# Sums of weight blocks for a seven-product down projection: made by accumulating transfers in DRAM instead of by GpSimd in SBUF

## The chip, the core and the metric

One core of a Trainium2 chip runs the whole program. The metric is device time in microseconds. The kernel before takes 1990.42 us, the median of 3 runs (1988.92 to 1992.81). One more execution was taken with the profiler; all rows below are from that one.

Engines, as the profile names them: PE is the matrix engine (PEld its weight loads), DVE the vector engine, ACT the scalar engine, POOL is GpSimd, SP the engine that only issues transfers. SP, ACT and POOL each issue transfers on a queue of their own (q1, q10 and q0 in the profile), and all three queues are served by the same 16 DMA engines. Each engine works through its own instructions in order; an instruction that waits for a semaphore holds up all that stand behind it on that engine.

## What is computed

Two layers, each a token mixer and a gated channel MLP, on x of 512 tokens by 1024 channels, float32:

```python
for i in range(DEPTH):                       # DEPTH = 2
    mix = mixer_sublayer(x, w_in[i], ...)    # input projection, pooling mixer, SSD mixer, gates, w_out
    x = layer_norm(ALPHA * x + mix, ...)
    h = dwconv_centred(x @ w_up[i], ...)     # 1024 -> 2 * 2816
    gate, val = split(h)
    x = layer_norm(ALPHA * x + (gelu(gate) * val) @ w_down[i], ...)   # 2816 -> 1024
```

The change concerns the last product, (512 x 2816) @ (2816 x 1024), and only the way in which its weights are prepared.

## The kernel before

**Matmuls in three parts.** Every float32 operand of the big products is split into a rounded part h and a remainder l; `mm3` (L378 to L383) issues three matmuls, h·h, h·l, l·h. The split of a weight tile (`WeightStream._split`, L77 to L92) is an ACT cast (L90, `wh`) and a DVE subtraction (L91, `wl`) of 128 x 1024 values.

**The weight stream.** A plan lists raw loads of up to 1 MB (`wraw`, two buffers) and the order in which their pieces are split. SP issues the loads, `_split` cuts them two tiles ahead of PE, three `wh`/`wl` buffers hold them.

**The down projection with seven products.** `strassen_projection` (L604) multiplies 2 x 2 blocks of activations and weights with seven products instead of eight (Strassen's scheme in Winograd's form). The 2816 rows of `w_down` are 22 row blocks of 128; each of the 11 pairs has two row blocks and two halves of 512 columns, so four blocks b00, b01, b10, b11 per pair. Four products need sums of these blocks. Before the change `StrassenWeights` (L107) makes them on POOL when a pair's tile has been loaded: per pair three subtractions of 128 x 512 (L137, L138 in place in the loaded tile, L126 into the space of the old activations, `xths`/`xtls`), and later, for two pairs at once, one subtraction of 128 x 1024 (L154). The raw load of a pair has b00, b01 and b11 (768 KB); b10 comes later in three loads of up to 1 MB.

The stage has two parts: in the first, PE does four products for each of 11 pairs (24 matmuls a pair), while the other activation sums come back from DRAM (`asp`, `fetch` L618) and are cut again (`cut` L621, L624 and L625); in the second, the remaining three products.

**What sets the order of the work around the change.** PE's program order is the order of the source. The other engines' order is set by the framework's scheduler, which places an instruction where it takes the engine to be free and its inputs to be there; it may move one far ahead of the place where it was written. In the mixer, POOL makes the decay masks (`affine_select` of `m`, L994; `m` is loaded from DRAM on ACT's queue, L989), and per unit of four heads `xw` (L1051), `y` (L1057), state products `s` (L1076) and the sums into `y` (L1109). ACT exponentiates `m` (L1001) after the masks. PE's state product `stp` (L1068) reads `xw`, its `ydp` (L1019) reads `m`, its `yop` (L1095) reads `s`. In names like `m_0_775` the first number is the head, in `xw_0_826`, `y_0_829` and `s_0_2_921` the unit; the last one only numbers the buffer.

Of the kernel before, what the change touches and what calls it, by code (L numbers as in the profile page):

```python
# [9 lines left out]
F32 = mybir.dt.float32  # L10
# [3 lines left out]
ALU = mybir.AluOpType  # L14
# [3 lines left out]
P = 128  # L18
T = 512
D = 1024  # L20
KD = D // P
# [17 lines left out]
class WeightStream:  # L39
# [3 lines left out]
    def __init__(self, nc, tc, pool, plan, ahead, raw_bufs, bufs):  # L43
        self.nc, self.tc, self.pool = nc, tc, pool
        self.plan = plan
        self.subs = [(i, j) for i, r in enumerate(plan) for j in r["order"]]
        self.ahead = ahead
        self.raw_bufs, self.bufs = raw_bufs, bufs
        self.raw = {}
        self.done = {}  # L50
        self.next_raw = 0
        self.next_sub = 0
        self.pos = 0
        self.seq = []
        self.extra = {}
# [51 lines left out]
class StrassenWeights:  # L107
# [4 lines left out]
    def __init__(self, nc, tc, pairs):  # L112
        self.nc, self.tc, self.pairs = nc, tc, pairs
        self.t2 = {}
        self.raw0 = None

    def open(self, tiles):

        for t in tiles:
            for i in range(t.shape[1]):  # L120
                self.t2[len(self.t2)] = (t, i)
        self.make_t2(0, self.raw0)

    def make_t2(self, i, raw):
        t, j = self.t2[i]
        self.nc.gpsimd.tensor_tensor(  # L126
            t[:, j, :], raw[:, 1024:1536], raw[:, 512:1024], op=ALU.subtract
        )

    def direct(self, raw):  # L130

        return raw.rearrange("p (a b) -> p a b", a=2)[:, :, 0:512]

    def sums(self, i, raw):

        g = self.nc.gpsimd
        g.tensor_tensor(raw[:, 1536:2048], raw[:, 1024:1536], raw[:, 512:1024], op=ALU.subtract)  # L137
        g.tensor_tensor(raw[:, 512:1024], raw[:, 512:1024], raw[:, 0:512], op=ALU.subtract)  # L138
        if i:
            self.make_t2(i, raw)  # L140
        else:
            self.raw0 = raw
        return raw.rearrange("p (a b) -> p a b", a=2)[:, :, 512:1024]

    def two(self, q):
        t, j = self.t2[2 * q]
        return t[:, j : j + min(2, self.pairs - 2 * q), :]

    def lower(self, q, o, raw):

        t = self.two(q)
        n = t.shape[1]
        b = raw[:, o : o + n * 512].rearrange("p (a b) -> p a b", a=n)
        self.nc.gpsimd.tensor_tensor(t, b, t, op=ALU.subtract)  # L154
        return b

    def plan(self, w, first):

        raws, direct, sums = [], [], []
        for i in range(self.pairs):  # L160
            a, b = 2 * i * P, (2 * i + 1) * P
            raws.append({"srcs": [w[a : a + P, :].unsqueeze(1),
                                  w[b : b + P, 512:1024].unsqueeze(1)], "order": range(2)})
            direct.append((first + i, self.direct))
            sums.append((first + i, partial(self.sums, i)))
        seq = []
        for i in range(self.pairs - 2):
            seq += [direct[i], sums[i]]
        seq += direct[-2:] + sums[-2:]
        odd = w.rearrange("(k two p) c -> two p k c", two=2, p=P)[1, :, :, 0:512]  # L170
        lower, t2, t4 = [], [], []
        for i in range(0, self.pairs, 4):
            n = min(4, self.pairs - i)
            r = first + len(raws)
            raws.append({"srcs": [odd[:, i : i + n, :]], "order": range(n)})
            for k in range(0, n, 2):
                q = (i + k) // 2
                lower.append((r, partial(self.lower, q, k * 512)))
                t2.append((r if q else r - 1, lambda raw, q=q: self.two(q)))
                t4.append((r, lambda raw, q=q: self.two(q)))  # L180
        nq = len(t2)
        for q in range(nq - 2):
            seq += [t2[q], lower[q]]
        return raws, seq + t2[-2:] + lower[-2:] + t4
# [40 lines left out]
def weight_plan(l, w_in, pool_w, w_ssd_proj, w_out, w_up, w_down, down):  # L225
# [71 lines left out]
    r, s = down.plan(w_down[l], len(raws))  # L297
# [4 lines left out]
def tile_hybrid_pool_ssd_convffn_encoder(  # L302
# [60 lines left out]
    downs = [StrassenWeights(nc, tc, KF // 2) for _ in range(NL)]  # L363
# [134 lines left out]
    class Norm:  # L498
# [28 lines left out]
        def add(self, c, c0, ps, first=False, last=False):  # L527

            c1 = c0 + ps.shape[1]
            xs = self.xcs[c][:, c0:c1]  # L530
            if first:
                nc.vector.scalar_tensor_tensor(xs, xs, ALPHA, ps, op0=ALU.mult, op1=ALU.add)
            else:
                nc.vector.tensor_tensor(xs, xs, ps, op=ALU.add)
            if last:
                self.stats(c, c0, c1)
# [67 lines left out]
    def strassen_projection(l, name, sw, tags, pool, spill, norm):  # L604
# [13 lines left out]
        def fetch(i):  # L618
            nc.sync.dma_start(again[:, i % 2], spill[i])

        def cut(i):  # L621
            h = pool.tile([P, 4, 256], F32R, tag=f"ah{i}", name=f"{name}h{i}")
            lo = pool.tile([P, 4, 256], F32R, tag=f"al{i}", name=f"{name}l{i}")
            nc.scalar.copy(h[:, :3], again[:, i % 2])  # L624
            nc.vector.tensor_tensor(lo[:, :3], again[:, i % 2], h[:, :3], op=ALU.subtract)  # L625
            second[i] = (h, lo)
# [19 lines left out]
        for i in range(n - 2):  # L646
# [11 lines left out]
            fetch(i)  # L658
# [14 lines left out]
        for i in (n - 2, n - 1):  # L673
            both(yb, (tags[i], 1), s[i - n + 2], 0, False, i == n - 1)
            both(zb, (tags[i], 2), s[i - n + 2], 1, False, i == n - 1)
            fetch(i)
            cut(i - 1)
# [24 lines left out]
        with tc.high_priority():  # L702
            for cc in range(2):
                norm.add(cc, 512, xb[cc])
                norm.add(2 + cc, 512, xb[cc])
            if final:
                norm.add(3, 256, xb[1][:, 256:512])
# [60 lines left out]
    for l in range(NL):  # L768
# [483 lines left out]
        for g in range(4):  # L1252
# [88 lines left out]
        for j in range(KF):  # L1341
# [22 lines left out]
            nc.vector.tensor_tensor(q[:, 1], a21, r[:, 1], op=ALU.add)  # L1364
            nc.vector.tensor_tensor(q[:, 2], q[:, 0], a21, op=ALU.subtract)
            nc.vector.tensor_tensor(r[:, 2], q[:, 1], q[:, 0], op=ALU.subtract)
            nc.vector.tensor_tensor(q[:, 3], r[:, 0], r[:, 2], op=ALU.subtract)
# [57 lines left out]
```

## Time and profile before

| what | us |
|---|---|
| median of 3 runs | 1990.42 |
| profiled execution, its own time | 1992.83 |
| its span in the trace | 1991.0 |
| PE busy | 1931.9 (97%) |
| DVE busy | 1348.4 (68%) |
| ACT busy | 998.4 (50%) |
| POOL busy | 609.0 (31%) |

The span is one execution from its first to its last instruction; the stages follow each other in it: mixer of layer 0 to about 578 us, output projection and norm to about 636 us, up projection to 872 us, down projection to about 995 us, and the same again for layer 1, whose down projection runs from about 1868 us to the end. Idle time of an engine costs something only where the engine that sets the end waits for it.

### The profile page before, as it was taken

Reading aid. Unit: us, or ns where it says so; the run is one execution under the profiler, and the core shown is the slowest. Engines: PE = TensorE matmul, PEld = TensorE weight load, DVE = VectorE, ACT = ScalarE, POOL = GpSimd, SP = SyncE. Lnnn points to the kernel's source line nnn. Section 1 sums busy time; section 2 is a strip of 40 time slices with the busy share of each in tenths; the row PEclk is TensorE's granted clock in tenths of the full one; section 3 lists DMA queues with packets and bytes.
Section 4 is the critical chain, followed back from the end, with each engine's and each line's share of the span. In section 5 each row is a group of like instructions: output and inputs, shape, how many; then the busy total and the mean of one; then the engine's idle time right before and its main releaser. Section 6 shows DMA issues by size and latency. Waiting matters only on the chain.

```text
span 1991.0 us, 27368 instructions
## 1 busy us (share of the span) xinstructions
PE 1931.9 (97%) x10449; PEld 1616.0 (81%) x10449; DVE 1348.4 (68%) x1945; ACT 998.4 (50%) x1665; POOL 609.0 (31%) x578
## 2 busy tenths in 40 slices
PE   8999999999999999998999999999999999999997
PEld 7878798988888888876788878989888888888765
DVE  5668576775556656679985685667656566666898
ACT  4767666644333444444457776656443334444443
POOL 1244424241111111168303343242411111111773
PEclk9999999999999999999999999999999999999999
DMA  5444434233241334345225344343332414333541
GB/s 159 123 119 117 127 93 140 86 113 115 76 164 49 121 112 134 106 153 190 83 90 160 106 112 124 110 124 105 85 111 92 168 43 130 121 101 116 180 154 51
DMA packets 174691, 232.19 MB, mean 117 GB/s; under 512 B 7872, under 2 KB 128868, under 8 KB 174560
## 3 DMA queue, kind: packets, MB, share of 16 engines
q1 hardware_dynamic: 152144, 178.80, 28.3%
q10 hardware_dynamic: 17712, 34.08, 7.0%
q0 software_dynamic: 4704, 17.56, 2.5%
q8 instruction: 83, 1.36, 0.3%
q14 instruction: 48, 0.39, 0.1%
HBM read 217.31 MB, written 13.11 MB: 116 GB/s over the span
## 4 chain that ended last, share of the span: by engine, by line
PE 78%; DVE 6%; issue 6%; POOL 4%; DMA 3%; ACT 3%; SPq 0%; POOLq 0%; ACTq 0%; DVEq 0%
PE fg L382 7%; PE fg L381 7%; PE fg L383 7%; PE spp L381 3%; PE zp L381 3%; PE spp L382 3%; PE spp L383 3%; PE zp L382 3%; PE zp L383 3%; PE xp L381 3%; DVE wl L91 3%; PE xp L383 3%; PE xp L382 3%; PE stp L1068 2%; PE ydp L1019 2%
## 5 line engine op out<-in xcount | busy, mean ns | idle before, releaser
L91 DVE TENSOR_TENSOR wl<-wraw,wh 128x1024 fp32r<-128x1024 f32 (+1 forms) x330 | 454.1, 1377 | 251.6 <-ACT wh L90 250.0
L90 ACT CAST wh<-wraw 128x1024 fp32r<-128x1024 f32 (+1 forms) x330 | 341.2, 1035 | 503.6 <-PE fg L382 158.0
L383 PE MATMUL fg<-xthm,wl 128*128 128x512 f32 x640 | 249.0, 389 | 0.0
L381 PE MATMUL fg<-xthm,wh 128*128 128x512 f32 x640 | 249.0, 389 | 0.0
L382 PE MATMUL fg<-xtlm,wh 128*128 128x512 f32 x640 | 249.0, 389 | 0.0
L1001 ACT ACTIVATE m<-m,nac 128x128 f32<-128x128 f32 x512 | 159.6, 392 | 52.2 <-POOL m L994 51.7
L994 POOL TENSOR_SCALAR_AFFINE_SELECT m<-m 128x512 f32<-128x512 f32 x128 | 95.0, 765 | 183.5 <-DMA m<-acd 162.9
L381 PEld LDWEIGHTS fg<-xthm,wh 128*128 128x128 f32 x640 | 120.1, 188 | 25.0
L383 PEld LDWEIGHTS fg<-xthm,wl 128*128 128x128 f32 x640 | 120.1, 188 | 24.9
L382 PEld LDWEIGHTS fg<-xtlm,wh 128*128 128x128 f32 x640 | 120.1, 188 | 24.9
L1109 POOL TENSOR_TENSOR y<-y,yo 128x256 f32<-128x256 f32 x96 | 85.4, 898 | 101.6 <-DVE yo L1101 98.8
L381 PE MATMUL spp<-yth,wh 128*128 128x512 f32 x256 | 110.3, 431 | 0.5 <-ACT yth L1149 0.5
L382 PE MATMUL spp<-ytl,wh 128*128 128x512 f32 x256 | 101.2, 395 | 0.7 <-DVE ytl L1150 0.7
L383 PE MATMUL spp<-yth,wl 128*128 128x512 f32 x256 | 101.1, 395 | 0.0
L479 DVE SCALAR_TENSOR_TENSOR xc<-xp,pcwc,xc 128x510 f32<-128x510 f32 (+1 forms) x128 | 95.2, 745 | 7.2 <-ACT xc L473 5.7
L1002 DVE TENSOR_TENSOR m<-m 128x512 f32<-128x512 f32 x64 | 46.7, 730 | 64.8 <-ACT m L1001 55.5
L1051 POOL TENSOR_TENSOR xw<-xtok,wst 128x768 f32<-128x768 f32 x32 | 51.3, 1621 | 121.9 <-ACT xtok L943 99.0
L1363 POOL TENSOR_TENSOR r<-cvv,cg 128x512 f32<-128x512 f32 x22 | 28.4, 1292 | 175.1 <-issue 130.4
L381 PE MATMUL zp<-wh,xthf 128*128 128x256 f32 x256 | 77.6, 303 | 0.0
L1286 POOL TENSOR_TENSOR g<-g,acc 128x512 f32<-128x512 f32 x16 | 27.5, 1720 | 162.3 <-ACT g L1247 150.3
L381 PE MATMUL zp<-wh,xthi 128*128 128x256 f32 x256 | 77.1, 301 | 0.0
L382 PE MATMUL zp<-wl,xthf 128*128 128x256 f32 x256 | 73.0, 285 | 0.0
(403 smaller groups left out, 5214.0 us busy)
## 6 DMA issues: line engine op xcount, KB each, us to landing
wraw<-in_w_in_dram SPq DMA_DIRECT2D x56, 1024.0 KB, 5.5
wraw<-in_w_up_dram SPq DMA_DIRECT2D x44, 1024.0 KB, 5.2
m<-acd ACTq DMA_DIRECT2D x64, 512.0 KB, 4.9
wraw<-in_w_ssd_proj_dram SPq DMA_DIRECT2D x16, 1024.0 KB, 5.1
wraw<-in_w_down_dram SPq DMA_DIRECT2D x22, 512.0 KB, 3.6
asp<-r POOLq DMA_DIRECT2D x22, 384.0 KB, 2.9
xtls<-asp SPq DMA_DIRECT2D x22, 384.0 KB, 3.8
wraw<-in_w_in_dram SPq DMA_DIRECT2D x16, 512.0 KB, 5.3
```

The source lines that it names most:

```text
L90: self.nc.scalar.copy(hv, src)
L91: self.nc.vector.tensor_tensor(lv, src, hv, op=ALU.subtract)
L381: mm(lhsT=ah, rhs=bh, start=first, stop=False)
L382: mm(lhsT=ah, rhs=bl, start=False, stop=False)
L383: mm(lhsT=al, rhs=bh, start=False, stop=last)
L479: nc.vector.scalar_tensor_tensor(dst[:, o0:o1], ps[:, o0 + s : o1 + s], tap, dst[:, o0:o1], op0=ALU.mult, op1=ALU.add,)
L994: nc.gpsimd.affine_select(out=mv, in_=mv, pattern=[[0, NCH], [1 - 2 * d, P]], compare_op=ALU.is_ge, fill=NEG, base=0, channel_multiplier=2 ...
L1001: nc.scalar.activation(mc, mc, AF.Exp, bias=nac[:, c, col : col + 1])
L1002: nc.vector.tensor_tensor(m[:, 0], m[:, 0], m[:, 1], op=ALU.add)
L1019: nc.tensor.matmul(ps[q * 64 : (q + 1) * 64, c * 64 : (c + 1) * 64], lhsT=m[:, 0, t0 : t0 + 64], rhs=xtok[:, c, hh * 64 : (hh + 1) * 64], ...
L1051: nc.gpsimd.tensor_tensor(h4(xw[:, d]), h4(xtok[:, d : d + 3, :]), hb(wst, d, d + 3, d), op=ALU.mult)
L1109: nc.gpsimd.tensor_tensor(y[:, c, :], y[:, c, :], yo[:, d, :], op=ALU.add)
```

## The change

The sums of blocks are made before the stage needs them, in DRAM, by transfers that POOL issues and that add to what lies at their destination. `StrassenWeights.prepare(step)` is written in the mixer's loop over four groups: in step 0, four copies of all 11 blocks of a kind (b01, b01, b11, b10) to a DRAM tile `wsum`; in step 1, two accumulating transfers (b00 onto the first, b11 onto the second); in steps 2 and 3 one each, from one part of `wsum` onto another. Each transfer is 1408 rows of 2 KB, 2.88 MB; there are 8 per layer, 16 in all. The down projection then loads 1 MB per pair (b00, b11 and two sums), later one sum and b10 for two pairs at a time, and the last sum for four pairs. POOL does none of the sums any more. Since the transfers can only add, some sums have the other sign, and a few DVE instructions subtract where they added. The space of the old activations becomes two more raw buffers (`raw_at`) and five buffers for `asp` instead of two.

```diff
     def _load(self, i):
         r = self.plan[i]
-        raw = self.pool.tile([P, 2048], F32, tag="wraw", name=f"wraw{i}", bufs=self.raw_bufs)
+        if i in self.raw_at:
+            raw = self.raw_at[i]
+        else:
+            raw = self.pool.tile([P, 2048], F32, tag="wraw", name=f"wraw{i}",
+                                 bufs=self.raw_bufs)
...
-    def make_t2(self, i, raw):
...
-    def sums(self, i, raw):
...
-    def lower(self, q, o, raw):
...
+    def __init__(self, nc, w, pairs, sums):
+        self.nc, self.pairs, self.sums = nc, pairs, sums
+        self.blocks = w.rearrange("(k two p) (h c) -> two h p k c", two=2, h=2, p=P)
+
+    def _put(self, t, src, op=None):
+        dst = self.sums[:, :, t, :]
+        if op is None:
+            self.nc.gpsimd.dma_start(dst, src)
         else:
...
+            self.nc.gpsimd.dma_start(dst, src, accum_op=op)
+
+    def prepare(self, step):
+
+        b, t = self.blocks, self.sums
+        if step == 0:
+            for n, (i, j) in enumerate(((0, 1), (0, 1), (1, 1), (1, 0))):
+                self._put(n, b[i, j])
+        elif step == 1:
+            self._put(0, b[0, 0], ALU.add)
+            self._put(1, b[1, 1], ALU.add)
+        else:
+            self._put(step, t[:, :, 0 if step == 2 else 2, :], ALU.add)
...
+        for i in range(n):
+            raws.append({"srcs": [b[0, 0, :, i : i + 1, :], b[1, 1, :, i : i + 1, :],
+                                  t[:, i, 0:2, :]], "order": range(2)})
+            direct.append((first + i, view(0)))
+            sums.append((first + i, view(1024)))
...
+    downs = [
+        StrassenWeights(nc, w_down[l], KF // 2,
+                        dram.tile([P, KF // 2, 4, 512], F32, name=f"wsum{l}"))
+        for l in range(NL)
+    ]
...
-        sw.open([scratch[0], scratch[1][:, : n - KD, :]])
-        again = scratch[1][:, 3:6, :].rearrange("p a b -> p (a b)").rearrange(
-            "p (s a b) -> p s a b", s=2, a=3)
+        more = scratch[0].rearrange("p a b -> p (a b)").rearrange("p (s b) -> p s b", s=2)
+        for i in range(ws.next_raw, ws.next_raw + n - 2):
+            if (i - ws.next_raw) % 4 < 2:
+                ws.raw_at[i] = more[:, i % 2]
+        again = scratch[1].rearrange("p a b -> p (a b)")[:, : 5 * 768].rearrange(
+            "p (s a b) -> p s a b", s=5, a=3)
...
-            norm.add(2 + cc, 512, zb[cc])
+            norm.add(2 + cc, 512, zb[cc], op=ALU.subtract)
...
                 make_bc(g, feature_tiles(f"bc{l}_{g}_", 2))
+            downs[l].prepare(g)
             ujobs.append(unit(2 * g))
```

The change moves instructions on POOL. First place: POOL in layer 0, from the last parameter loads to the first head masks (`dsk` is a parameter load, `wsum_83` the DRAM tile of layer 0, `wsum_84` that of layer 1; in brackets the semaphores that a row waits for, `DMASW` those of POOL's own transfers, eight of them, taken in turn). Before:

```order
L785 DMA dsk_158<-in_d_skip_dram 128x32 [waits DMASW1_49]
L781 DMA dtb_8530<-in_dt_bias_dram 128x64 [waits DMASW7_49,DMASW2_49,DVE_49]
L783 DMA nea_8532<-in_a_log_dram 128x64 [waits DMASW3_49,DVE_49]
L1057 TENSOR_TENSOR y_0_829<-xtok_0_424,dsk_158 128x1024 [waits DMASW1_49,Activation_49]
L994 AFFINE_SELECT m_0_775<-m_0_775 128x512 [waits DMAHW6_49]
L994 AFFINE_SELECT m_0_775<-m_0_775 128x512
L1051 TENSOR_TENSOR xw_0_826<-xtok_0_424,wst_752 128x768 [waits DVE_49]
```

With the change, the same place:

```order
L782 DMA dsk_160<-in_d_skip_dram 128x32 [waits DMASW1_49]
L127 DMA wsum_83<-in_w_down_dram 1408x1x512 [waits DMASW2_49]
...
L127 DMA wsum_83<-in_w_down_dram 1408x1x512 [waits DMASW5_49]
L129 DMA wsum_83<-in_w_down_dram 1408x1x512 [waits DMASW6_49,DMASW2_49]
L129 DMA wsum_83<-in_w_down_dram 1408x1x512 [waits DMASW7_49,DMASW3_49]
L129 DMA wsum_83<-wsum_83 1408x512 [waits DMASW6_49,DMASW4_49,DMASW0_49]
L991 AFFINE_SELECT m_0_781<-m_0_781 128x512 [waits DMAHW6_49]
```

Seven of layer 0's eight transfers now stand ahead of the first mask, though they were written in steps 0 to 2; the fifth waits for the first to land, the seventh for the third and the fifth.

Second place: POOL just behind that, after the masks of heads 0 to 2 and `xw` and `y` of unit 0, with the change (before, `s_0_2` follows `xw_0` at once):

```order
L1054 TENSOR_TENSOR y_0_835<-xtok_0_430,dsk_160 128x1024 [waits DMASW1_49]
L129 DMA wsum_83<-wsum_83 1408x512 [waits DMASW5_49,DMASW0_49]
L1073 TENSOR_TENSOR s_0_2_927<-s_0_1_908,tot_769 128x512 [waits Activation_49]
L778 DMA dtb_8525<-in_dt_bias_dram 128x64
L780 DMA nea_8527<-in_a_log_dram 128x64
L127 DMA wsum_84<-in_w_down_dram 1408x1x512
```

The eighth transfer of layer 0 waits for the seventh, ahead of unit 0's state product, and layer 1's first copy follows in layer 0.

Third place: POOL around the heads 9 and 10 of layer 0, with the change. Layer 1's other copies and two accumulating transfers stand a little ahead of this; what follows is its last two:

```order
L1073 TENSOR_TENSOR s_1_3_1505<-s_1_2_1432,tot_769 128x512 [waits DVE_49]
L129 DMA wsum_84<-wsum_84 1408x512 [waits DMASW6_49,DMASW2_49,DMASW0_49]
L991 AFFINE_SELECT m_10_1524<-m_10_1524 128x512 [waits DMAHW5_49,PE_49]
...
L1106 TENSOR_TENSOR y_1_1260<-y_1_1260,yo_1_2_1617 128x256 [waits Pool_49]
L129 DMA wsum_84<-wsum_84 1408x512 [waits DMASW7_49,DMASW3_49,DMASW2_49]
L1106 TENSOR_TENSOR y_1_1260<-y_1_1260,yo_1_0_1655 128x256 [waits DVE_49]
L1106 TENSOR_TENSOR y_1_1260<-y_1_1260,yo_1_3_1672 128x256 [waits DVE_49]
L1048 TENSOR_TENSOR xw_2_1764<-xtok_2_1150,wst_758 128x768 [waits Activation_49]
```

The last transfer of all, the sixteenth, is issued between sums into `y` of unit 1 and `xw` of unit 2, and waits for the one ahead of it to land. In the mixer of layer 1 POOL has none of these transfers.

## Rows read from the trace of the kernel before

**Rows 1.** The page, busy time of each engine: us (share of the span) and instructions.
```profile
PE 1931.9 (97%) x10449; PEld 1616.0 (81%) x10449; DVE 1348.4 (68%) x1945; ACT 998.4 (50%) x1665; POOL 609.0 (31%) x578
```

**Rows 2.** Stretches: us, then PE, PEld, DVE, ACT, POOL busy, clock, DMA share, GB/s.
```profile
871.90:943.00 71.10, 63.38 (x256) 48.23 (x255) 66.09 (x41) 31.90 (x35) 61.20 (x36) 0.98 0.62 199
...
1868.00:1926.00 58.00, 50.23 (x207) 37.77 (x206) 56.51 (x31) 25.64 (x28) 52.55 (x28) 1.00 0.59 190
```

**Rows 3.** DVE's groups by form, 868 to 995 us: busy us, mean ns, idle before.
```profile
L91 DVE TENSOR_TENSOR wl<-wraw,wh 128x1024 fp32r<-128x1024 f32 x26 | 53.1, 2043 | 5.3 <-ACT wh L90 5.0
L625 DVE TENSOR_TENSOR dp_l<-xtls,dp_h 128x768 fp32r<-128x768 f32 x11 | 21.0, 1912 | 0.5 <-ACT dp_h L624 0.5
```

**Rows 4.** The same view of DVE, 636 to 868 us (up projection of layer 0).
```profile
L91 DVE TENSOR_TENSOR wl<-wraw,wh 128x1024 fp32r<-128x1024 f32 x42 | 51.6, 1230 | 49.3 <-ACT wh L90 49.3
```

**Rows 5.** DVE in order of time, down projection of layer 0: start us, us, what.
```profile
902.44 4.55 DVE L91 TENSOR_TENSOR wl<-wraw,wh 128x1024 fp32r<-128x1024 f32 x2
...
908.89 4.54 DVE L91 TENSOR_TENSOR wl<-wraw,wh 128x1024 fp32r<-128x1024 f32 x2
...
943.28 0.96 DVE L625 TENSOR_TENSOR dp_l<-xtls,dp_h 128x768 fp32r<-128x768 f32 x1 [0.47 <-ACT dp_h L624]
```

**Rows 6.** PE in order of time: first matmul of pairs 1 and 2, a later wait.
```profile
877.51 0.39 PE L381 MATMUL dp_v<-wh,ah 128*128 128x512 f32 x1
...
883.08 0.39 PE L381 MATMUL dp_v<-wh,ah 128*128 128x512 f32 x1
...
891.93 0.51 PE L382 MATMUL dp_v<-wl,ah 128*128 128x512 f32 x1 [1.15 <-DVE wl L91]
```

**Rows 7.** DMA queues, 872 to 943 us: packets, MB, share of 16 engines.
```profile
q1 hardware_dynamic: 4742, 12.53, 54.7%
```

**Rows 8.** DMA queues over the whole span (the page).
```profile
q10 hardware_dynamic: 17712, 34.08, 7.0%
```

**Rows 9.** POOL in order of time, layer 0's mixer; idle before and what ended it.
```profile
11.04 0.55 POOL L783 DMA_DIRECT2D nea<-in_a_log_dram  x1 [3.21 <-DMA pcwc<-in_ssd_conv_w_dram]
...
71.40 1.22 POOL L994 TENSOR_SCALAR_AFFINE_SELECT m<-m 128x512 f32<-128x512 f32 x2 [0.97 <-DMA m<-acd]
...
82.73 1.19 POOL L1076 TENSOR_TENSOR s<-s,tot 128x512 f32<-128x512 f32 x1 [4.45 <-ACT s L1074]
...
157.07 4.79 POOL L1109 TENSOR_TENSOR y<-y,yo 128x256 f32<-128x256 f32 x5
166.13 2.91 POOL L1051 TENSOR_TENSOR xw<-xtok,wst 128x768 f32<-128x768 f32 x2 [4.28 <-ACT xtok L943]
```

**Rows 10.** The chain that ended last, 55 to 170 us: start us, us, what.
```profile
78.26 0.86 PE stp L1068 x4
...
121.45 3.36 POOL xw L1051 x2
124.85 0.73 PE stp L1068 x2
```

**Rows 11.** ACT in order of time, layer 0's mixer.
```profile
72.06 0.70 ACT L1001 ACTIVATE m<-m,nac 128x128 f32<-128x128 f32 x2 [2.32 <-POOL m L994]
...
86.18 1.98 ACT L90 CAST wh<-wraw 128x1024 fp32r<-128x1024 f32 x2
```

**Rows 12.** Stretches of layer 0's mixer, columns as in rows 2.
```profile
0.00:20.00 20.00, 12.30 (x69) 11.12 (x70) 5.73 (x7) 6.24 (x8) 8.26 (x51) 1.00 0.93 282
20.00:60.00 40.00, 40.00 (x289) 36.75 (x289) 29.39 (x50) 22.21 (x31) 1.07 (x2) 1.00 0.20 58
60.00:164.00 104.00, 100.45 (x692) 87.31 (x689) 63.96 (x89) 77.71 (x159) 42.31 (x44) 0.98 0.49 129
12.00:14.00 2.00, 2.00 (x11) 2.00 (x10) 0.77 (x1) 1.00 (x1) 0.11 (x1) 1.00 1.03 397
```

**Rows 13.** POOL's groups by line, whole span: issue of a 128-row transfer.
```profile
L1368 POOL DMA_DIRECT2D asp<-r x22 | 12.9, 584 | 31.3 <-DVE q L1367 26.9 <-issue 4.4
```

More of the change, by code (lines that the diff above doesn't have):

```diff
@@ L49, in __init__ @@
         self.raw = {}
+        self.raw_at = {}
         self.done = {}
@@ L107 @@
 class StrassenWeights:
[L112 to L122, printed above, removed]
-    def make_t2(self, i, raw):
[L125 to L128, printed above, removed]
@@ L145, in two @@
-    def two(self, q):
-        t, j = self.t2[2 * q]
-        return t[:, j : j + min(2, self.pairs - 2 * q), :]
-    def lower(self, q, o, raw):
[L151 to L157, printed above, removed]
-        raws, direct, sums = [], [], []
[L160 to L165, printed above, removed]
+    def __init__(self, nc, w, pairs, sums):
+        self.nc, self.pairs, self.sums = nc, pairs, sums
+        self.blocks = w.rearrange("(k two p) (h c) -> two h p k c", two=2, h=2, p=P)
@@ new lines, in plan, with view @@
+    def plan(self, first):
+        n, b, t = self.pairs, self.blocks, self.sums
+        raws, direct, sums = [], [], []
+        def view(o, n=2):
+            return lambda raw: raw[:, o : o + n * 512].rearrange("p (a b) -> p a b", a=n)
+        for i in range(n):
[3 more added lines that the diff above has]
+            sums.append((first + i, view(1024)))
@@ L166, in plan @@
         seq = []
-        for i in range(self.pairs - 2):
+        for i in range(n - 2):
             seq += [direct[i], sums[i]]
         seq += direct[-2:] + sums[-2:]
-        odd = w.rearrange("(k two p) c -> two p k c", two=2, p=P)[1, :, :, 0:512]
         lower, t2, t4 = [], [], []
[L172 to L180, printed above, removed]
@@ L181, in plan @@
-        nq = len(t2)
-        for q in range(nq - 2):
+        for i in range(0, n, 2):
+            m = min(2, n - i)
+            t2.append((first + len(raws), view(0, m)))
+            lower.append((first + len(raws), view(m * 512, m)))
+            raws.append({"srcs": [t[:, i : i + m, 2, :], b[1, 0, :, i : i + m, :]],
+                         "order": range(2)})
+        for i in range(0, n, 4):
+            m = min(4, n - i)
+            for k in range(0, m, 2):
+                t4.append((first + len(raws), view(k * 512, min(2, m - k))))
+            raws.append({"srcs": [t[:, i : i + m, 3, :]], "order": range(2)})
@@ L183, in plan @@
+        for q in range(len(t2) - 2):
             seq += [t2[q], lower[q]]
@@ L296, in weight_plan @@
         seq += [a[0], b[0], a[1], b[1]]
-    r, s = down.plan(w_down[l], len(raws))
+    r, s = down.plan(len(raws))
     return raws + r, seq + s
@@ L525, in root, with add @@
             return y
-        def add(self, c, c0, ps, first=False, last=False):
+        def add(self, c, c0, ps, first=False, last=False, op=ALU.add):
             c1 = c0 + ps.shape[1]
@@ L531, in add @@
             if first:
-                nc.vector.scalar_tensor_tensor(xs, xs, ALPHA, ps, op0=ALU.mult, op1=ALU.add)
+                nc.vector.scalar_tensor_tensor(xs, xs, ALPHA, ps, op0=ALU.mult, op1=op)
             else:
-                nc.vector.tensor_tensor(xs, xs, ps, op=ALU.add)
+                nc.vector.tensor_tensor(xs, xs, ps, op=op)
             if last:
@@ L623, in cut @@
             lo = pool.tile([P, 4, 256], F32R, tag=f"al{i}", name=f"{name}l{i}")
-            nc.scalar.copy(h[:, :3], again[:, i % 2])
-            nc.vector.tensor_tensor(lo[:, :3], again[:, i % 2], h[:, :3], op=ALU.subtract)
+            nc.scalar.copy(h[:, :3], again[:, i % 5])
+            nc.vector.tensor_tensor(lo[:, :3], again[:, i % 5], h[:, :3], op=ALU.subtract)
             second[i] = (h, lo)
@@ L657, in strassen_projection @@
                 both(xb, (tags[i], 0), d, 0, f, False)
-            fetch(i)
+            for j in range(i + 3 if i else 0, min(i + 4, n)):
+                fetch(j)
             if i:
@@ L703, in strassen_projection @@
             for cc in range(2):
-                norm.add(cc, 512, xb[cc])
-                norm.add(2 + cc, 512, xb[cc])
+                norm.add(cc, 512, xb[cc], op=ALU.subtract)
+                norm.add(2 + cc, 512, xb[cc], op=ALU.subtract)
             if final:
```

17 lines of the change are left out of this document (3 added, 14 removed).

## The prediction

> **What bounds the kernel now.** The page's first part says that PE is busy for 97% of the span [rows 1]. So only two things can move the time: a stretch in which PE waits now and would not, or one in which it would begin to wait. The view of busy time by stretch finds the first kind: in the first part of the down projection of layer 0 PE works 63.38 of 71.10 us, in that of layer 1 50.23 of 58.00 [rows 2]. The idle time is 7.7 and 7.8 us, 15.5 together, and DVE is busy for nearly all of both stretches.
>
> DVE's groups tell why. A subtraction `wl` takes 2043 ns there, and the activation remainder (L625) 1912 [rows 3]; in the up projection the same `wl` takes 1230 [rows 4]. DVE in order of time shows a pair after pair: two `wl` of 4.55 us together, then L625, and the next pair begins 908.89 - 902.44 = 6.45 us later; once POOL has finished its sums, L625 takes 0.96 [rows 5]. PE needs 883.08 - 877.51 = 5.57 us for a pair when nothing holds it, and later waits 1.15 us for a `wl` [rows 6]. So POOL's sums do not hold PE by their own length, they stretch DVE's work from 2 x 1.23 + 0.96 = 3.4 us a pair to 6.45.
>
> The Trainium skill, "SBUF — State Buffer", section "Who interferes with whom", says that a DVE instruction with two SBUF inputs and a GpSimd instruction that reads SBUF block each other outright; the stretched rows agree.
>
> **The change, part by part.** *The sums leave POOL.* DVE falls to 3.4 us a pair, under PE's 5.57, so PE bounds both stretches and the 15.5 us of idle go; I take 15, since the first tiles still have to be cut. What is late next would be the loads: a pair now moves 1.05 MB of weights and 0.39 MB of `asp`. On q1 the trace moved 12.53 MB in 54.7% of 71 us, 323 GB/s [rows 7]; 1.44 MB at that rate are 4.5 us of 5.57. With four raw buffers this is hidden, cost 0; if that cover failed, the 15 us would shrink.
>
> *The signs.* The same number of DVE instructions, the operation alone differs: 0. *More buffers for `asp`*: fetches go out earlier, 0, under the same 4.5 us.
>
> *Sixteen transfers in layer 0's mixer.* This is the term that decides. By the order of instructions all sixteen stand in the mixer of layer 0, the first seven ahead of the first mask, the last between `y` of unit 1 and `xw` of unit 2; each accumulating one waits until the transfers on whose data it works have landed. Such a wait holds POOL: before the change POOL stands still 3.21 us ahead of the load of `nea` until an earlier load has landed [rows 9]. Behind POOL stand the masks, then ACT's exponentials, and behind these ACT's casts of weights: ACT waits for the first mask for 2.32 us and casts the next tiles after the exponentials [rows 11]. PE's state product follows directly on `xw` in the chain of waits: `xw` ends at 124.8 and `stp` starts at 124.85 [rows 10]. So nearly every microsecond by which POOL is late there goes to PE.
>
> When are the transfers done? All queues use the same 16 engines, so I add up work. The engines are 93% busy until 20 us [rows 12]; I let the new work start there, though its first transfers are issued soon after 12 us. *A copy* is 2.88 MB; at 323 GB/s it takes 8.9 us. No row shows a transfer from DRAM to DRAM. The lower end is the best stretch of loads, 397 GB/s [rows 12], 7.3 us. *A sum* reads two blocks and writes one. The lower end is one copy at the best rate, 7.3 us. The upper end is three passages one after another at the slowest rate of a large queue, q10's 34.08 MB in 7.0% of 1991 us, 245 GB/s [rows 8], 35.4 us. I take two readings at 323 GB/s, 17.8 us, since in the rows of loads the write of what is read costs nothing visible; the row of the down projection's loads, with rows of 2 and 4 KB as here, is the nearest.
>
> The Trainium skill, "Collectives: The Full Stack", section "The bandwidth ceiling: the fold count and why AG ≠ RS ≠ AR", says that a reducing transfer is slower than a copy because of its two source reads, 1.93 times in its measurement; by that a sum is 17.2 us and the total 4 us less. No run here shows it.
>
> The sixteenth transfer is issued when fifteen have gone through, 8 copies and 7 sums: 8 x 8.9 + 7 x 17.8 = 196 us. Beside them go the loads that the mixer needs anyway: 58 GB/s for 40 us and 129 GB/s for 104 us [rows 12], 2.3 + 13.4 = 15.7 MB, at 323 GB/s 49 us. So it is issued at 20 + 196 + 49 = 265 us. Without cost it could be issued until two sums into `y` (0.96 us each, 4.79 / 5) ahead of `xw` of unit 2 at 166.13 [rows 9], at 164. **POOL, and PE behind it, is 101 us late there.** The earlier waits lie on the same path and are not added. The seventh transfer, behind four copies and one sum, is issued at 20 + 35.6 + 17.8 + 12 (3.7 MB of other loads) = 85 where the first mask started at 71.40 [rows 9]; the eighth, two sums and 6 us of other loads later, at 127 where `s` started at 82.73. The lateness grows 14, 44, 101.
>
> *The issue on POOL.* 584 ns for a transfer of 128 rows [rows 13]. The new ones have 1408 rows: 0.6 us each if the length doesn't matter, 11 times as much, 6.4 us, if it does. Seven of them, 45 us, fit between 12 us and the first mask; the other nine, up to 58 us, fit into the waits. Cost 0, and 58 if the waits are gone.
>
> *Collisions with weights and `m`.* They are in the sum, which counts the engines' work of all queues. After the sixteenth transfer the rest of layer 0 and the mixer of layer 1 are as before.
>
> **The sum.** 101 - 15 = 86 us more. The profiled execution took 1992.83 us (span 1991.0), 2.4 above the median; from the median, 1990.4 + 86 = 2076, and I say 2075.
>
> **Rivals.** *The transfers are done in time.* If a sum costs no more than a copy and both run at 397 GB/s, fifteen take 109 us, the other loads 40, and the sixteenth is issued at 169: 5 us late, 1990 + 5 - 15 = 1980, and 1975 if the start at 12 us makes up for them. For it: the engines are only 20% busy from 20 to 60 us [rows 12]. Against it: it needs the best two microseconds of the trace for two hundred. It decides below about 8 us per transfer. This is the other side: faster.
>
> *A sum costs one copy at 323 GB/s.* 15 x 8.9 + 49 + 20 = 203, 39 us late, 2014. For it: reads and writes of the engines overlap in all rows; against: a second source has to be read.
>
> *Dearer sums.* At 35.4 us each: 20 + 71 + 248 + 49 = 388, 224 us late, 2199. For it: q10's reads of DRAM run at 245 GB/s [rows 8]; against: that queue moves broadcasts beside two others.
>
> The Trainium skill, "DMA: Bandwidth & Descriptors", section "Latency and other measured facts", gives 214 GB/s as the full rate of copies between HBM tensors; by that a copy is 13.5 us, a sum of two readings 27, the sixteenth transfer is issued at 366, and the time would be about 2177. No row here shows such a copy.
>
> *The change does not do what it says:* it was written for four steps of each mixer, and by the order it happens early in layer 0 alone; that is the forecast's cause, not another case. That the down projection doesn't gain its 15 us would add 15 to every case.
>
> **How the numbers follow.** Forecast (late by some 60 to 150 us) 0.50; sums for the price of a copy 0.15; dearer 0.19; in time 0.12; between in time and one copy, so that loss and gain cancel, 0.04. The range has to reach from the dearer case to the one in time: 1976 to 2200. Less than 0.2% (4 us) can't be told from no change. Faster is the case in time, 0.12; same 0.04; slower the rest, 0.84. Nearly all cases but one slow the kernel, so the range is wide because the price of a sum is not in the trace.
>
> **What would show it.** Right: PE idle by tens of microseconds between 70 and 270 us, POOL waiting on transfers into `wsum` ahead of the first masks, of `s` of unit 0 and of `xw` of unit 2; `wl` at about 1.23 us in both down projections and a pair every 5.6 us. Wrong: PE busy throughout the first 200 us; sums that land within 9 us; POOL busy instead of waiting; or a down projection that waits for `wraw`.

## The result, and the profile after

The changed kernel takes **2105.48 us**, median of 4 runs (2099.38 to 2107.06), against 1990.99 (1988.92 to 1992.81, 4 runs) for the kernel before: ratio 1.057, 95% interval 1.055 to 1.059. The profiled execution has a span of 2104.6 us, 113.6 more than before. In the page the shares of PE and DVE fall [rows 1], and q0, which makes the transfers, moves 63.70 MB where it moved 17.56 before:

```profile
PE 1946.8 (93%) x10449; PEld 1631.5 (78%) x10449; DVE 1287.5 (61%) x1945; ACT 1000.3 (48%) x1666; POOL 464.6 (22%) x516
...
q0 software_dynamic: 21856, 63.70, 12.1%
```

**Where the time went: layer 0's mixer.** Busy time by stretch of the changed kernel, columns as in rows 2:

```profile
20.00:60.00 40.00, 28.91 (x186) 25.88 (x185) 17.23 (x28) 11.94 (x16) 3.47 (x2) 0.87 1.02 319
60.00:164.00 104.00, 77.25 (x503) 66.06 (x501) 50.58 (x70) 52.33 (x98) 25.66 (x29) 0.90 1.03 224
164.00:276.00 112.00, 51.40 (x328) 44.98 (x328) 33.59 (x46) 39.70 (x74) 25.91 (x28) 0.71 0.89 210
276.00:400.00 124.00, 111.74 (x629) 92.00 (x630) 77.63 (x141) 72.35 (x159) 39.33 (x40) 0.93 0.51 125
```

From 20 to 164 us the engines' share is over 1.0, where it was 0.20 and 0.49 [rows 12], and PE is idle for part of each stretch. Its granted clock falls to a mean of 0.71 while it idles, so that some of what it still does runs at the 1.2 GHz level.

POOL in order of time, same kernel; compare rows 9:

```profile
37.83 1.76 POOL L129 DMA_DIRECT2D wsum<-in_w_down_dram  x1 [21.93 <-DMA wsum<-in_w_down_dram]
...
86.64 1.51 POOL L129 DMA_DIRECT2D wsum<-wsum  x1 [36.07 <-DMA wsum<-in_w_down_dram]
...
98.13 1.22 POOL L991 TENSOR_SCALAR_AFFINE_SELECT m<-m 128x512 f32<-128x512 f32 x2 [9.98 <-DMA m<-acd]
...
126.97 1.51 POOL L129 DMA_DIRECT2D wsum<-wsum  x1 [12.29 <-DMA wsum<-wsum]
...
182.31 1.23 POOL L991 TENSOR_SCALAR_AFFINE_SELECT m<-m 128x512 f32<-128x512 f32 x2 [27.80 <-DMA m<-acd]
...
272.92 1.51 POOL L129 DMA_DIRECT2D wsum<-wsum  x1 [23.95 <-DMA wsum<-wsum]
...
275.20 3.50 POOL L1048 TENSOR_TENSOR xw<-xtok,wst 128x768 f32<-128x768 f32 x2
```

The seventh transfer goes out at 86.6, the eighth at 127.0, the sixteenth at 272.9, and `xw` of unit 2 behind it at 275.20 instead of 166.13 [rows 9]: 109 us late. But POOL does not wait for transfers alone: it waits 133 us for them (the first and the last line here) and 96 for loads of `m`. The waits of the first 320 us (us in all, times, longest):

```profile
POOL wsum L129 <- DMA wsum<-in_w_down_dram: 97.0, 4, 36.1
POOL m L991 <- DMA m<-acd: 96.2, 13, 27.8
...
PE stp L1065 <- POOL xw L1048: 59.1, 6, 26.0
ACT wh L95 <- DMA wraw<-in_w_in_dram: 45.3, 9, 15.2
...
POOL wsum L129 <- DMA wsum<-wsum: 36.2, 2, 23.9
```

In the kernel before, over the same time, PE waited 3.2 us for `xw`, ACT 5.0 for these weights, and POOL for `m`:

```profile
POOL m L994 <- DMA m<-acd: 57.9, 14, 9.8
```

In the chain that ended last, from 20 to 300 us of the changed kernel, landings of the new transfers make 27.5%, and landings of `m` and of weights 26.1%. The first mask shows how the two go together. The wait for transfers ends at 86.64, but ACT had waited for weights, and so the first load of `m` goes out only then; ACT's longest such wait, and that load with the change and before it:

```profile
46.60 1.05 ACT L95 CAST wh<-wraw 128x1024 fp32r<-128x1024 f32 x1 [15.21 <-DMA wraw<-in_w_in_dram]
...
86.79 0.40 ACTq L986 DMA_DIRECT2D m<-acd  x1
```

```profile
65.92 0.40 ACTq L989 DMA_DIRECT2D m<-acd  x1
```

The mask at 98.13, 27 us late, would have been as late if POOL had waited for no transfer (in e6 below, where it waits for none, it starts at 97.97).

**What a transfer costs.** The queues from 20 to 56 us, when q0 still has some of its first four copies (11.5 MB) to move (packets, MB, share of 16 engines), and what a weight load then takes:

```profile
q0 software_dynamic: 2407, 9.60, 77.8%
...
wraw<-in_w_in_dram SPq DMA_DIRECT2D x2, 1024.0 KB, 25.8
```

and from 88 to 126 us, when q0 carries sums:

```profile
q0 software_dynamic: 2164, 4.37, 63.4%
```

9.60 MB in 77.8% of 36 us are 343 GB/s, 8.4 us for a copy of 2.88 MB; 4.37 MB in 63.4% of 38 us are 181 GB/s, **15.9 us for a sum**. All sixteen are 8 x 8.4 + 8 x 15.9 = 194 us of all 16 engines. (The expectations below reckon with 9.6 us a copy and 204 in all, from 32 to 66 us, a stretch that reaches into the first sum.)

**The down projections gained 6.7 us, not 15.** `wl` and the activation remainder (now L622) take what was forecast; DVE's groups from 989 to 1116 us, beside rows 3:

```profile
L96 DVE TENSOR_TENSOR wl<-xths,wh 128x1024 fp32r<-128x1024 f32 x10 | 12.2, 1225 | 8.0 <-ACT wh L95 8.0
L622 DVE TENSOR_TENSOR dp_l<-xtls,dp_h 128x768 fp32r<-128x768 f32 x11 | 10.5, 958 | 9.7 <-ACT dp_h L621 9.7
```

But PE stands still once in each layer, at the second pair, for 5.6 us in layer 0 and 2.8 in layer 1. PE, ACT and SP's queue in order of time in layer 0:

```profile
1003.74 0.80 PE L375 MATMUL dp_v<-wh,ah 128*128 128x512 f32 x1 [5.63 <-ACT wh L95]
```

```profile
1002.64 1.04 ACT L95 CAST wh<-xths 128x1024 fp32r<-128x1024 f32 x1 [3.10 <-DMA xths<-in_w_down_dram]
```

```profile
992.31 0.33 SPq L616 DMA_DIRECT2D xtls<-asp  x1
992.68 2.79 SPq L71 DMA_DIRECT2D xths<-in_w_down_dram  x4
```

`xths` is the scratch that holds the old activations; PE's last `fg` matmul read them until 992.5, so the second pair's weights can't be fetched earlier, while weights of later pairs already went into raw buffers. The idle time then pulls the clock down (last column but two):

```profile
1000.00:1004.00 4.00, 0.27 (x1) 0.27 (x1) 1.22 (x3) 1.12 (x2) 0.00 (x0) 0.54 0.99 370
1004.00:1008.00 4.00, 3.54 (x8) 2.47 (x9) 3.20 (x4) 3.40 (x4) 1.09 (x2) 0.50 0.55 188
```

### The profile page after: what moved, and what is told of

The parts are those of the page before. It is cut to its first block, busy times and chain, and to the rows that moved or that the text cites. A ratio compares the mean times of both kernels' runs of the same rounds, so it can differ in the third digit from the quotient of the medians.

```text
span 2104.6 us, 27337 instructions
## 1 busy us (share of the span) xinstructions
PE 1946.8 (93%) x10449; PEld 1631.5 (78%) x10449; DVE 1287.5 (61%) x1945; ACT 1000.3 (48%) x1666; POOL 464.6 (22%) x516
## 3 DMA queue, kind: packets, MB, share of 16 engines
q1 hardware_dynamic: 161328, 196.10, 29.5%
q0 software_dynamic: 21856, 63.70, 12.1%
HBM read 280.75 MB, written 59.24 MB: 162 GB/s over the span
## 4 chain that ended last, share of the span: by engine, by line
PE 75%; DMA 9%; issue 8%; DVE 3%; POOL 2%; ACT 1%; SPq 0%; ACTq 0%; POOLq 0%; DVEq 0%
PE fg L377 7%; PE fg L376 7%; PE fg L375 7%; PE spp L375 3%; PE spp L376 3%; PE spp L377 3%; PE zp L375 2%; PE zp L376 2%; PE zp L377 2%; DMA wsum<-in_w_down_dram 2%; DMA m<-acd 2%; PE xp L375 2%; PE xp L377 2%; PE stp L1065 2%; PE xp L376 2%
## 5 line engine op out<-in xcount | busy, mean ns | idle before, releaser
L96 DVE TENSOR_TENSOR wl<-wraw,wh 128x1024 fp32r<-128x1024 f32 (+1 forms) x334 | 415.3, 1246 | 319.1 <-ACT wh L95 317.9
L1065 PE MATMUL stp<-xw,btok 128*128 128x256 f32 x192 | 54.8, 406 | 62.4 <-POOL xw L1048 62.2
L1065 PEld LDWEIGHTS stp<-xw,btok 128*128 128x128 f32 x192 | 36.0, 199 | 71.3 <-POOL xw L1048 66.1
L557 POOL TENSOR_TENSOR x<-x,lnb 128x512 f32<-128x512 f32 x15 | 22.6, 1511 | 307.2 <-DVE x L553 293.3
## 6 DMA issues: line engine op xcount, KB each, us to landing
wsum<-in_w_down_dram POOLq DMA_DIRECT2D x12, 2816.0 KB, 49.1
wsum<-wsum POOLq DMA_DIRECT2D x4, 2816.0 KB, 29.5
```

Source lines behind the costliest of these rows:

```text
L96: self.nc.vector.tensor_tensor(lv, src, hv, op=ALU.subtract)
L1065: nc.tensor.matmul(ps[:, d * 256 : (d + 1) * 256], lhsT=btok[:, c, :], rhs=xw[:, d, c - d, :], start=True, stop=True,)
```

## The experiments

Two theories of the mixer's loss stood against each other. **T**: POOL's waits for transfers to land, set by where the transfers stand, hold the masks. **C**: the transfers' work on the 16 engines delays the loads of `m` and of weights, whoever waits. All times are medians of 4 to 10 runs beside runs of the kernel before (1989.86 to 1990.77).

| kernel | us | ratio to before, 95% interval |
|---|---|---|
| no transfers (e3) | 1981.57 | 0.996 (0.995 to 0.997) |
| no transfers, scratch moved (e4) | 1970.24 | 0.990 (0.988 to 0.991) |
| a transfer behind every fourth mask (e1) | 2067.59 | 1.039 (1.037 to 1.040) |
| same, scratch moved (e2) | 2058.34 | 1.034 (1.033 to 1.036) |
| early, copies that wait for nothing (e6) | 2072.22 | 1.041 (1.039 to 1.043) |
| cut small in the mixers, scratch moved (e8) | 2026.42 | 1.018 (1.016 to 1.019) |
| whole in the up projections, scratch moved (e7) | 2040.37 | 1.025 (1.024 to 1.027) |
| same, plain copies (e10) | 1989.97 | 1.000 (0.999 to 1.001) |
| same as e7, sums further apart (e11) | 2012.06 | 1.010 (1.008 to 1.012) |
| cut small in the up projections, scratch moved (e9) | **1972.54** | 0.992 (0.990 to 0.993) |

e3, e4, e6 and e10 leave out the forming of the sums: other blocks stand in their place, and only their time is of use.

### The down stage by itself (e3, e4)

e3 drops the transfers and loads plain blocks in place of the sums (the first of three such loads is shown); e4 also (the last two lines) gives the first two of every four loads to the raw buffers, the next two to the scratch.

```diff
-            downs[l].prepare(g)
...
-                                  t[:, i, 0:2, :]], "order": range(2)})
+                                  b[0, 1, :, i : i + 1, :], b[1, 0, :, i : i + 1, :]], "order": range(2)})
...
-            if (i - ws.next_raw) % 4 < 2:
+            if (i - ws.next_raw) % 4 >= 2:
```

> Leaves out the forming of the sums: no transfer at all, and the down projection loads plain blocks of w_down where it would load the sums, of the same size and shape. This is the down stage's part of the change alone. By the changed kernel's stage starts the two down projections give 2.2 + 4.5 = 6.7 us: 1984. By the forecast's term of 15 us: 1976. If the down stages lose beside the transfers (rival C in another place), it would be below 1984 by what they lose.

> Leaves out the forming of the sums, as the kernel without transfers, and gives the first two loads of each down projection to the raw buffers instead of the scratch. If the scratch, free only behind the last fg matmul, makes the second pair late: 1976, 8 us below the kernel without transfers. If the second pair is late for another reason: as that one, 1984.

Measured: 1981.57 and 1970.24; moving the scratch is worth 11.3 us. The start of layer 0's down projection in e3 and then in e4, by stretch:

```profile
870.00:882.00 12.00, 7.58 (x31) 5.61 (x30) 6.09 (x8) 3.60 (x4) 3.42 (x5) 0.98 0.92 299
882.00:886.00 4.00, 3.70 (x11) 2.59 (x9) 0.16 (x2) 2.56 (x4) 1.08 (x2) 0.64 0.89 294
```

```profile
870.00:882.00 12.00, 12.00 (x53) 9.74 (x52) 8.94 (x11) 6.75 (x8) 3.41 (x5) 1.00 0.95 315
882.00:886.00 4.00, 4.00 (x19) 3.25 (x18) 1.61 (x3) 2.37 (x3) 1.08 (x2) 1.00 0.96 366
```

The wait and the low clock are gone with the scratch's place. Both down stages, from the first `dp_v` to the next layer's first matmul (layer 0) and from the last `fg` to the last `dp_w` (layer 1), in us:

| | before | after | e3 | e4 |
|---|---|---|---|---|
| layer 0 | 123.0 | 120.8 | 119.1 | 112.0 |
| layer 1 | 120.3 | 115.8 | 117.3 | 112.1 |

So the sums' leaving POOL is worth 19.2 us once the scratch is out of the way, and 6.9 with it in the way.

### Transfers that nobody has to wait for (e1, e2, e6)

e1 puts eight transfers into each layer's own mixer, one behind every fourth mask; e2 is e1 with e4's edit; e6 (the lines behind the dots) leaves them early and makes two independent copies of each sum.

```diff
+                    if h % 4 == 0 and h < 32:
+                        with tc.issue_after(masks[0].ins):
+                            downs[l].transfer(h // 4)
...
-            self._put(step, t[:, :, 0 if step == 2 else 2, :], ALU.add)
+            for n in range(2):
+                self._junk(2 * step + n, b[n, 1 - n])
```

> The same sixteen transfers, but eight in each layer's own mixer, one behind the mask of every fourth head (h = 0, 4, ... 28), so that each has some 50 us before the next and none stands ahead of the masks. Theory T (POOL waits early in layer 0 for transfers to land, and masks, xw and PE behind them): POOL no longer waits for a transfer, the mixers of both layers are as in the kernel before, and only the down stages' gain of 6.7 us is left: 1991 - 7 = 1984, with 8 issues of 1 to 2 us in each mixer at most 1995. Rival C (the transfers' work on the 16 engines starves the loads of weights and of m, whoever waits on POOL): the transfers are 8 x 9.6 + 8 x 15.9 = 204 us of the engines' full share, and the kernel with the change lost 120 us beside them, 0.59 us for each; the same loss again, 2100, or half of it where the engines have more room, 2045.

> As the one with a transfer behind every fourth mask, and the first two loads of the down projection's weights go to the four raw buffers instead of the scratch that holds old activations until the last fg matmul. Theory T, with the second pair's stall laid to the scratch: the second pair no longer waits for ACT's cast wh, the clock stays at its upper level, and the down stages give their whole idle time, 15 us instead of 6.7: about 8 us below the kernel without this edit, 1976. Rival: the second pair waits for something else (the fetches of asp, DVE's wl), and the time is that of the kernel without this edit, within 2 us. Rival C as there: above 2040 with or without it.

> As the changed kernel, but each of the eight accumulating transfers is two plain copies into a DRAM tile of their own: no transfer works on what another has written, so POOL waits for none, and the engines' work is 24 copies x 9.6 = 230 us instead of 204. It leaves out the forming of the sums (blocks stand in their place). Theory T (POOL's waits for landings make the loss): POOL is free, the transfers are all issued early, and most of the 120 us of the mixer go: under 2030. Rival C (the engines' work starves the loads of m and of the weights, whoever waits): the masks wait for m instead, and the loss stays: 2080 to 2130.

Measured: 2067.59, 2058.34, 2072.22. Against the kernels without transfers the loss is 86 us (e1 against e3), 88 (e2 against e4) and 91 (e6 against e3), where the changed kernel lost 2105.48 - 1981.57 = 124. Theory T falls as the main cause: in these three POOL never waits for a transfer to land, and some 70% of the loss or more stays (91 of 124 us in e6). e1 on POOL behind its first transfer:

```profile
96.61 1.05 POOL L127 DMA_DIRECT2D wsum<-in_w_down_dram  x1
99.86 1.22 POOL L1002 TENSOR_SCALAR_AFFINE_SELECT m<-m 128x512 f32<-128x512 f32 x2 [2.21 <-DMA m<-acd]
...
113.50 0.63 POOL L1002 TENSOR_SCALAR_AFFINE_SELECT m<-m 128x512 f32<-128x512 f32 x1 [11.71 <-DMA m<-acd]
```

and its stretches:

```profile
108.00:112.00 4.00, 2.67 (x12) 1.88 (x10) 0.00 (x0) 1.94 (x4) 0.00 (x0) 1.00 0.89 240
112.00:116.00 4.00, 0.67 (x3) 0.67 (x4) 1.14 (x3) 1.83 (x6) 1.91 (x3) 0.64 0.94 230
116.00:120.00 4.00, 4.00 (x12) 3.22 (x11) 2.99 (x4) 3.27 (x6) 2.23 (x3) 0.50 0.29 65
```

While the copy fills the engines, a load of `m` issued at 100.54 takes 12.8 us to land (the median was 4.9 before), and POOL waits 11.71 us for it. A sum into `y` stands behind the mask, DVE's next `y` waits for that, PE stands still from 110.7 to 115.3, and its next 4 us are at a clock of 0.50. In e6 the first mask starts at 97.97 instead of 71.40 [rows 9], though POOL waits for no transfer: ACT waits for weights for 53.1 us of the first 320 (5.0 before), so that the first load of `m` goes out at 88.75 instead of 65.92, and takes 9.2 us to land. What e6 does remove is PE's wait for `xw`:

```profile
PE stp L1071 <- POOL xw L1054: 15.2, 4, 8.5
```

instead of 59.1. Its copies run at 341 GB/s (8.94 MB in 77.2% of 34 us), so its 24 copies are 24 x 8.5 = 203 us of the engines, not 230 as expected, and close to the changed kernel's 194. With about that work kept and POOL's waits for landings gone, 2105 - 2072 = 33 us of the 124 go and 91 stay. This does not split the loss cleanly: in e6 waits for `m` and for weights stand where POOL's waits for landings stood.

### The same transfers in the up projections (e7, e10)

PE is never idle there before the change and no `m` is loaded. e7 puts a whole transfer behind every even j; e10 (behind the dots) drops the adding.

```diff
+                if i < 8:
+                    with tc.issue_after(last.ins):
+                        downs[l].transfer(i)
...
-            self._put(n - 4, b[n - 4, n - 4], ALU.add)
+            self._put(n - 4, b[n - 4, n - 4])
```

> The sixteen transfers in another stage: eight in each layer's own up projection, one behind POOL's product a21 of every even j from 0 to 14, some 21.8 us apart, and the first two loads of the down projection's weights in the raw buffers. In the mixer the transfer behind every fourth mask cost 85 us beside the kernel without transfers, though POOL waited for none. Theory C' (a transfer fills the 16 engines for 10 to 18 us, and what it delays is the load of m, which has three buffers and stands ahead of masks, exponentials and tiles): in the up projection there is no m, PE is never idle there in the kernel before, and the weights come 4 loads ahead in engines busy for 0.38 of the time, so the transfers cost nothing: 1970, as without transfers, at most 1980 with the stores of asp late behind them on the same queue. Rival C (any transfer costs PE some 0.4 us for each microsecond of the engines' work, wherever it stands, since the weights' loads are slowed too): 2050, as in the mixer.

> Leaves out the adding: as the kernel with whole transfers in the up projection, every even j from 0 to 14, but the four accumulating ones of each layer are plain copies of the same blocks to the same places. This prices the accumulation alone, with place, number, length in rows and spacing kept. Theory S: a copy of 9.6 us fits beside 8.2 + 2 us of loads in 21.8, so nothing is lost: 1970 to 1975. Rival (eight transfers of 2.88 MB in the up projection cost PE, whatever they do): 2040, as with the sums, or half of the 70 us, 2005.

Measured: 2040.37 and 1989.97, against 1970.24 without transfers: 70 and 20 us. e7 by stretch, four copies issued at 653 to 722, four sums at 746 to 834:

```profile
660.00:700.00 40.00, 40.00 (x178) 33.11 (x178) 22.18 (x29) 14.75 (x18) 7.25 (x9) 1.00 0.73 233
700.00:740.00 40.00, 40.00 (x177) 32.80 (x176) 22.71 (x30) 14.56 (x18) 6.14 (x7) 1.00 0.82 258
740.00:780.00 40.00, 32.11 (x128) 24.99 (x127) 18.90 (x24) 13.94 (x18) 8.14 (x8) 0.91 0.70 153
780.00:820.00 40.00, 35.61 (x149) 28.61 (x148) 20.98 (x27) 13.07 (x17) 6.70 (x7) 0.96 0.91 190
820.00:860.00 40.00, 29.33 (x116) 22.85 (x114) 14.04 (x18) 10.72 (x13) 4.79 (x5) 0.89 0.88 205
```

Nothing is lost beside these four copies; beside the sums PE waits for `wh`, and ACT for the weights (waits from 640 to 960 us):

```profile
ACT wh L95 <- DMA wraw<-in_w_up_dram: 62.3, 18, 9.8
...
PE fg L386 <- ACT wh L95: 22.3, 5, 6.9
```

The weights' loads land in 14.7 us (median, 655 to 860 us) where e4's take 5.1. So `m` isn't needed for the loss. The adding alone is 50 of the 70 us. Plain copies cost the other 20, where 0 to 5 were expected: e10's up projections take 222.6 and 224.1 us against e4's 217.6 and 217.7, and its down projections lose another 6. The price agrees: e10's q0 moves 27.00 MB in 40.9% of 215 us, 307 GB/s, a copy in 9.4 us; e7's moves 26.22 MB in 54.6% of 210 us, 114.7 us, of which 4 copies and 8 stores of `asp` take 48 at that rate, and four sums 66.7: 16.7 us each, 1.8 times a copy.

The Trainium skill, "Collectives: The Full Stack", section "The bandwidth ceiling: the fold count and why AG ≠ RS ≠ AR", has 1.93 between AllGather and ReduceScatter on a ring of cores and lays it to two source reads; a sum against a copy gives 1.9 (15.9 / 8.4) and 1.8 in the runs here, and no run shows the reason.

### How long one burst may be (e8, e11, e9)

e8 cuts each copy of the mixers into three pieces by rows, each sum into four, one piece a head; e11 keeps whole transfers but puts the sums of the up projection at j = 8, 11, 14, 17; e9 cuts copies into two and sums into three, one piece for each j from 0 to 19. All have the scratch moved. The lines are the cut (e8, e9), e9's place, for even and odd j, and e11's.

```diff
+            self.nc.gpsimd.dma_start(t[:, ks, n - 4, :], x[:, ks, :], accum_op=ALU.add)
...
+                if j < 20:
+                    with tc.issue_after(last.ins):
+                        downs[l].piece(j)
...
+                if j in (0, 2, 4, 6, 8, 11, 14, 17):
```

> The same transfers in the mixers, but cut by rows, a copy into three pieces and a sum into four, one piece behind the mask of each head from h = 0 to 27, and the first two loads of the down projection in the raw buffers. The engines' work is the same, its longest burst 3 to 4 us instead of 10 to 18. Theory C' (the length of a burst beside the slack of m's three buffers decides): the masks are late by a few us at most, and most of the loss goes: 1975 to 2000. Rival C (the sum of the work decides): no better than one whole transfer behind every fourth mask, 2058, and more with POOL's 28 issues of about 1 us.

> Whole transfers in the up projections again, but the accumulating ones 32.7 us apart instead of 21.8: the copies at j = 0, 2, 4, 6, the sums at j = 8, 11, 14 and 17. The cut transfers at 1972 had both shorter bursts and more time for the same work; this has the time alone: a sum of 15.9 us with three times 5 us of other loads in 32.7 us, a share of 0.95. If the engines' capacity decides (what a sum overfills is made up before the next): 1972 to 1982. If the length of a burst decides as well (weights' loads and asp's stores wait behind a whole sum): about as far above as the copies alone were, 1990, up to 2010.

> The transfers in the up projections, cut by rows: each copy into two pieces, each sum into three, one piece for each j from 0 to 19 (10.9 us apart). With whole transfers every 21.8 us PE lost nothing beside the copies of layer 0 and some 8 us beside each sum. Theory S (a sum of 15.9 us with 2 x 4.1 us of weights and 2 us of asp fills more than the 21.8 us that it has, so the weights' stock of four loads runs out): a third of a sum, 5.3 us, and 4.1 to 5 of other loads fit into 10.9 us, at a share of about 0.9, so PE loses little: 1970 to 1985, faster than the kernel before. Rival C (each microsecond of the engines' work beside PE costs 0.4, however it is cut): 2040, as with whole transfers.

Measured: 2026.42, 2012.06, 1972.54. Cutting alone takes the mixers' loss from 88 (e2) to 56 (e8): less than theory C' expected, so in the mixer both the burst and the sum of the work count. In the up projection e11 gives the sums half as much time again and still loses 42 us; e9, with the same work over the same time, but cut, loses 2. e11 and then e9, from 740 us:

```profile
740.00:780.00 40.00, 32.29 (x127) 25.04 (x126) 18.90 (x24) 12.60 (x16) 6.45 (x7) 0.87 0.69 161
```

```profile
740.00:780.00 40.00, 40.00 (x179) 33.10 (x178) 24.69 (x32) 16.36 (x21) 11.75 (x12) 1.00 0.89 210
780.00:820.00 40.00, 40.00 (x178) 33.14 (x177) 26.25 (x33) 17.96 (x22) 9.47 (x10) 1.00 0.89 212
820.00:860.00 40.00, 40.00 (x179) 33.10 (x177) 24.60 (x32) 18.00 (x22) 11.20 (x12) 1.00 0.87 199
```

```profile
wraw<-in_w_up_dram SPq DMA_DIRECT2D x17, 1024.0 KB, 5.6
```

e11's engines are 0.69 busy there (0.77 and 0.72 in the next two stretches) and PE starves; e9's are 0.89 busy, a weight load lands in 5.6 us (last line, e9), and PE is busy throughout. So the length of a burst, not the engines' capacity, decided there, for copies and sums alike: whole copies alone cost 20 [e10]. **e9 is the fastest version that does the whole computation: 17.3 us (0.8%) below the kernel before that ran beside it**, and 2 above the one that forms no sums (e4).

## Why the prediction was right, and where its steps were off

*The size and the sign* came out: 2105 against 2075, slower, and in layer 0's mixer. Step by step:

- **The sixteenth transfer at 265 us, POOL 101 late.** It went out at 272.9, `xw` was 109 late. The seventh and eighth, forecast at 85 and 127, went out at 86.6 and 127.0. The terms: a copy 8.9 forecast, 8.4 measured; a sum 17.8 forecast, 15.9 measured. Two readings at the loads' rate were a fair price. That the sixteenth came within 8 us is in part luck. The queues from 20 to 273 us:

```profile
q0 software_dynamic: 15630, 42.66, 72.8%
q1 hardware_dynamic: 11719, 10.75, 16.8%
q10 hardware_dynamic: 3072, 5.90, 7.6%
```

  Of the 253 us q0's fifteen transfers took 184 where the forecast had 196, and the other loads 62 where it had 49: the two errors cancel, and 7 us in which the engines had less than full work are left.
- **"So nearly every microsecond by which POOL is late there goes to PE."** The lateness was right, its cause only in part. The forecast let POOL's wait for landings carry the loss; e6, which has the work and no such wait, still loses 91 of 124 us, through late loads of `m` and of weights. The forecast came near because its term added up the engines' work of all queues, which is what both causes have in common. Already the first mask, 27 us late, was held by a late load of `m`, which the forecast had as work in its sum but not as a wait of its own. By its words e1 should have cost nothing; it cost 86.
- **"After the sixteenth transfer the rest of layer 0 ... as before."** PE's `op` of layer 0 starts 120.4 us late, 11 more than `xw`: the sixteenth still fills the engines behind 273 us, and PE works 111.74 of 124 us from 276 to 400, where it worked all of them before.
- **The down stage's 15 us: 6.7 measured.** This term failed, and by the cover that it named: "with four raw buffers this is hidden, cost 0". The loads' rate was enough; but the first two pairs behind the start load into a scratch that is free only when the up projection ends, while before the change all weights were loaded into `wraw` and only POOL's sums went into that scratch. e4 shows it: with the scratch used two pairs later the stages give 19.2. That is above the 15 because the rest of both stages, beyond rows 2, held another 4 us of idle time (50.31 of 52 and 50.71 of 53 us busy before).
- **POOL's issue at cost 0** held: 1.0 to 1.8 us for a transfer of 1408 rows, and e9 issues 40 pieces at 0.8 to 1.3 with about 2 us lost.
- **The rivals.** In time, and the price of one copy for a sum, fell by the 15.9 us; the dearer one too. The Trainium skill's 214 GB/s for copies between HBM tensors ("DMA: Bandwidth & Descriptors", section "Latency and other measured facts") led to the estimate of 2177; copies ran at 343, 307 and 341 GB/s here, so the measurement decides.

The sum: 109 + 11 late, less 6.7, is 113.3; the span grew by 113.6. The forecast was 2105.5 - 2075 = 30 us short: 8 at `xw`, 11 behind it and 8 in the down stages make 27, and the rest lies in the rounding to 2075 and between the profiled executions and the medians.

What stays open: whether the sums' extra time is the reading of what they add to, and how much of the loss is POOL's own waiting for landings: e6 says 33 us of 124, but it changes the transfers' kind along with their waits, and in the changed kernel's chain these waits are about as long as those for `m` and weights.

## What to carry to other kernels

Work moved from an engine to DMA isn't free because the queues look idle on average: price it in microseconds of all 16 engines, and ask which small load with few buffers (here `m`, then the weights) would stand beside each burst. Cut such transfers small and place them by hand where the other loads leave room; e9 and e11, in one stage with the same work, differ by 40 us. And when a change gives an old buffer a new use, ask when that buffer comes free: here a scratch came free too late.

## What the runs showed of the hardware

- An accumulating transfer between DRAM tensors takes 15.9 to 16.7 us of all 16 engines for 2.88 MB, a copy 8.4 to 9.4. The page's HBM counts rise by 46.1 MB written (59.24 against 13.11), which is the sixteen transfers, but by only 63.4 MB read (280.75 against 217.31), which is 46.1 for their sources and the 17.3 MB that are loaded besides: if a sum reads its own destination, that reading isn't in the count. Its longer time is in the engines' share all the same.
- With the engines full, a load of 1 MB took 25.8 us where it takes 5.1 to 5.5 otherwise, and the changed kernel's transfers from `w_down` took 49.1 us (median of 12) from issue to landing, those within `wsum` 29.5 (of 4).
